# Attention, convolution and filter sums in a two-layer encoder: four steps placed elsewhere in the order

## The chip, the cores and the metric

The kernel runs on one core of one Trainium2 chip. The metric is device time in microseconds (us) of one execution. Engines: PE is TensorE (its weight loads are shown as PEld), DVE is VectorE, ACT is ScalarE, POOL is GpSimd, SP is SyncE, which issues DMAs; POOL issues DMAs too.

## What is computed

The reference runs layers (here two, DEPTH = 2) on 1024 tokens of width 1024, all in float32. Each layer does three sub-layers, each followed by a residual sum and a layer norm:

```python
proj = x @ w_in
# (A) grouped-query attention, 8 query heads of 64 over 2 key/value heads, rotary
# (B) gated long convolution, 256 channels, by FFT with a filter that an MLP makes
# (C) latent attention, 4 heads, low-rank keys and values, rotary part apart
x = layer_norm(alpha * x + concat(A, B, C) @ w_o)
x = layer_norm(alpha * x + cross_attention(x, mem))      # 4 heads of 256, 256 memory tokens
x = layer_norm(alpha * x + moe(x))                       # 16 experts, each takes its top tokens
```

The kernel keeps float32 accuracy by splitting each matrix into a high part (rounded by a copy on ACT) and a low part (the difference, a subtraction on DVE or POOL) and multiplying in three passes. `split` is that pair of instructions: L175 the copy, L176 the subtraction; L187 to L189 are the three passes of a product.

## The kernel before

**Order.** PE, ACT and DVE execute their instructions in the order in which the program text issues them (MANUAL, L31, and `manual_schedule`, L2009). POOL and SP are not in MANUAL; the build orders them.

**Attention** (`attention`, L572) is one software pipeline over both kinds of heads: 48 pairs of 128-token blocks, 32 of grouped heads and then 16 of latent heads, two iterations a pair, so 96 iterations and some to drain. Iteration n issues, in this order:
- `put` of the pair that was finished: three copies `olo` from PSUM on ACT (L566 to L568), a sum and a product on POOL (L569, L570)
- in every second iteration the reciprocal `rd` of the two columns of sums `den` of one pair (L585, DVE). Before, that is the pair whose second half of values comes in this iteration: pair q at iteration 2q + 6
- the scores S of block n (L527, four matmuls for a grouped head, six for a latent one) and their row maximum `nm` (L530, DVE)
- `turn(n - 3)`: eight transposes of the exponentials (L544), split into `PH` (ACT) and `PL` (DVE), the operands of the value products
- exp of the scores (L536, ACT), which also sums the row into `den` (a second instruction reads the accumulator)
- half the values of an earlier pair (L554, L555); with the second half, two transposes of `rd` (L558), which `put` multiplies by
- `side(n, 2)`: what runs beside attention

**Beside attention**, in the order of `side`: one step of the convolution (`hyena`, L1001) if HYP(n) holds; a load of latent-attention tiles (`back`, L718, POOL's DMA queue) at iterations 57 to 63, 70, 78 and 86; a load of an out-projection weight `wo` (SP's queue) at 84, 86, ..., 96 and 97. The loads: Q tiles `mq` of the first block pair at 57, K tiles `mk` at 58 to 61, V tiles at 62 and 63, the other Q tiles at 70, 78 and 86; scores 64 are the first that need K, and scores 72, 80 and 88 the first that need the Q of 70, 78 and 86.

**The convolution** has one step outside the pipeline and 55 in it. Steps 1 to 8 are transposes and products on PE, with splits. Steps 9 to 46 are sums and products on POOL. Steps 47 to 50 and 52 are concerned with the inverse transform: a split `abh` (ACT), `abl` (POOL) of one block, and the load of the next table `tab` (L804, POOL's DMA queue); step 47 also reloads two tiles and the first table. Steps 49, 51, 53, 54 and 55 hold matmuls of the inverse. With the HYP of before, step 1 is at iteration 4, step 46 at 71, step 47 at 73, steps 48 to 50 at 74, 76 and 77, and step 55 at 85.

**The out-projection** follows: `Weight.get` splits a weight tile into `woh` (ACT) and `wol` (on DVE for `wo[0]` and `wo[2]`, on POOL for `wo[1]` and `wo[3]`) when it is first taken, before this is in the out-projection's first block. `r` (L1201) is the residual sum.

**Cross attention** runs 13 iterations over four heads: queries, scores, exponentials `xE` (L1389, ACT), the reciprocal of their sums (L1391, DVE), the product with it (L1392, POOL), transposes (L1403) with splits `xPH` and `xPL`, values. In layer 0 it also has the sums of the second layer's filter (`filter_later`, L943 to L997, 15 steps on DVE with an occasional copy): two steps after each iteration from 3 to 10.

Of the kernel before, what the change touches and what calls it, by code (L numbers as in the profile page):

```python
# [33 lines left out]
ML0 = 1  # L34
FM = 14
AT0 = 14
HYP = lambda n: n > 2 and n % 3
UC = 1
UG = 3
EM = 8  # L40
# [97 lines left out]
class Net:  # L138
# [433 lines left out]
    def attention(self, n_pairs, pair, side, lead=3):  # L572


        its = [(n, i) for n in range(n_pairs) for i in range(2)]
        E, PT, den, O, late, out = {}, {}, {}, {}, [], []
        for n in range(len(its) + lead + 3):
            for q in out:
                tp, _, _, f = pair(q)
                self.put(O.pop(q), tp, f)  # L580
            out = []
            if late and late[0][1]:
                q = late[0][0]
                rd = self.sml(2, "rd")
                self.nc.vector.reciprocal(rd, den[q])  # L585
                den[q] = rd
            sc = None
            if n < len(its):
                p, i = its[n]
                tp, passes = pair(p)[:2]  # L590
                sc = self.scores(passes(tp * 2 + i))
            side(n, 0)
            m = n - lead
            if 0 <= m < len(its):
                p, i = its[m]
                if i == 0:
                    PT[p] = ([self.big((128, 4, 256), F32R, name="PH") for _ in range(2)],
                             [self.big((128, 4, 256), F32R, name="PL") for _ in range(2)])
                self.turn(E.pop(m), *PT[p], i)
            side(n, 1)  # L600
            if sc:
                p, i = its[n]
                if i == 0:
                    den[p] = self.sp.tile([128, 2], F32, tag="den", name="den", bufs=6)
                E[n] = self.exps(*sc, den[p][:, i:i + 1])
            if late:
                q, half = late.pop(0)
                if half == 0:
                    O[q] = self.psO()
                self.values(O[q], *PT[q], den[q], pair(q)[2], half)  # L610
                if half:
                    out.append(q)
                    del PT[q], den[q]
            if 0 <= m < len(its) and its[m][1]:
                late += [(its[m][0], 0), (its[m][0], 1)]
            side(n, 2)
            yield
# [1139 lines left out]
    def run(self):  # L1757
# [26 lines left out]
        n = 0  # L1784
# [11 lines left out]
        for l in range(DEPTH):  # L1796
# [3 lines left out]
            wo = []  # L1800
            gqa, (mla, back) = self.gqa(), self.mla(l)
            hy = self.hyena(l)
            later = self.filter_later() if l == 0 else iter(())

            def side(n, at):
                if at != 2:
                    return
                if HYP(n):
                    next(hy, None)
                if 57 <= n < 64 or n in (70, 78, 86):  # L1810
                    next(back, None)
                if n in (84, 86, 88, 90, 92, 94, 96, 97):
                    wo.extend(self.out_weights(A["w_o"][l], [len(wo)]))

            ATS = 0
            att = self.attention(48, lambda n: gqa[n]() if n < 32 else mla[n - 32], side)
            for n, _ in enumerate(proj, NT if l else 0):
                if n == NT - 1 + (l > 0):
# [62 lines left out]
            for n, _ in enumerate(cross):  # L1881
                if n in (6, 7, 8, 9):
                    wo2 += self.out_weights(A["xa_wo"][l], [2 * (n - 6), 2 * (n - 6) + 1])
                for _ in range(WG.get(n, 0)):
                    next(w for w in wo2 if w.parts is None).get()
                if n == 11:
                    next(pl)
                if n >= 3:
                    next(later, None)
                    next(later, None)  # L1890

            self.more = True
            self.ew, loads = [], self.expert_weights(l)
# [142 lines left out]
```

## Time and profile before

| | |
|---|---|
| median of 3 runs | 2730.91 us (2730.67 to 2734.1) |
| the profiled execution | 2730.33 us, span 2728.6 us |
| PE busy | 2540.0 us, 93% of the span |
| DVE, ACT, POOL busy | 1963.7, 1589.2, 830.0 us (72%, 58%, 30%) |
| attention, layer 0 | scores 0 at 344.4 us, scores 95 at 655.8 us |
| attention, layer 1 | scores 0 at 1660.6 us, scores 95 at 1972.3 us |
| granted clock of PE, mean | 0.972 of 2.4 GHz |

A row of a timeline gives start, length, engine, line, operation, what it writes and reads with shapes, how many instructions are merged, and in brackets the idle time just before it and what ended that idle time. Ends of matmuls are modelled, and instructions of an engine overlap a little: the next may start before the last has left the pipe, so that the distance of two starts is the safer measure.

### The profile page before, as it was taken

Reading aid. Unit: us, or ns where it says so; the run is one execution under the profiler, and the core shown is the slowest. Engines: PE = TensorE matmul, PEld = TensorE weight load, DVE = VectorE, ACT = ScalarE, POOL = GpSimd, SP = SyncE. Lnnn points to the kernel's source line nnn. Section 1 sums busy time; section 2 is a strip of 40 time slices with the busy share of each in tenths; the row PEclk is TensorE's granted clock in tenths of the full one; section 3 lists DMA queues with packets and bytes.
Section 4 is the critical chain, followed back from the end, with each engine's and each line's share of the span. In section 5 each row is a group of like instructions: output and inputs, shape, how many; then the busy total and the mean of one; then the engine's idle time right before and its main releaser. Section 6 shows DMA issues by size and latency. Waiting matters only on the chain.

```text
span 2728.6 us, 39209 instructions
## 1 busy us (share of the span) xinstructions
PE 2540.0 (93%) x14132; PEld 2138.4 (78%) x14132; DVE 1963.7 (72%) x3089; ACT 1589.2 (58%) x2828; POOL 830.0 (30%) x761
## 2 busy tenths in 40 slices
PE   7899989999999895999989998999989999599998
PEld 5688879988778784777869887999877888477775
DVE  6765578877645678889876556887765356889887
ACT  4743379988123443887854425998732344377885
POOL 2412427963101201121131333688230130011112
PEclk9899999999999996999999999999999999799999
DMA  7545100333233357999975610005323235699994
GB/s 196 192 161 200 28 24 17 75 100 120 86 109 118 121 187 252 351 378 371 342 241 171 208 60 24 9 24 140 94 85 101 85 101 185 239 340 372 377 344 154
DMA packets 222581, 462.76 MB, mean 170 GB/s; under 512 B 26298, under 2 KB 83216, under 8 KB 222386
## 3 DMA queue, kind: packets, MB, share of 16 engines
q1 hardware_dynamic: 198402, 374.56, 39.2%
q0 software_dynamic: 19376, 68.91, 9.5%
q10 hardware_dynamic: 4608, 16.78, 1.5%
q8 instruction: 111, 1.82, 0.3%
q14 instruction: 84, 0.69, 0.1%
HBM read 369.75 MB, written 90.44 MB: 169 GB/s over the span
## 4 chain that ended last, share of the span: by engine, by line
PE 70%; DVE 13%; issue 5%; ACT 5%; DMA 4%; POOL 2%; SPq 0%; ACTq 0%; DVEq 0%; POOLq 0%
PE S L187 7%; PE S L188 7%; PE S L189 7%; PE S L527 6%; PE O L1709 6%; PE T L544 5%; PE O L189 5%; PE O L188 5%; PE O L187 5%; PE S L421 4%; PE O L555 3%; PE O L554 3%; DVE rk L1512 2%; DMA eg<-moe_w_up 1%; PE T L1463 1%
## 5 line engine op out<-in xcount | busy, mean ns | idle before, releaser
L176 DVE TENSOR_TENSOR egl<-eg,egh 128x1024 fp32r<-128x1024 f32 x256 | 305.8, 1221 | 49.9 <-ACT egh L175 45.6
L530 DVE TENSOR_REDUCE nm<-S 128x1 f32<-128x1024 f32 x192 | 234.5, 1223 | 102.5 <-PE S L527 100.4
L175 ACT ACTIVATE egh<-eg 128x1024 fp32r<-128x1024 f32 x256 | 265.1, 1058 | 41.0 <-PE S L188 23.9
L176 DVE TENSOR_TENSOR PL<-T,PH 128x512 fp32r<-128x512 f32 x384 | 246.3, 683 | 17.4 <-ACT PH L175 14.2
L175 ACT ACTIVATE PH<-T 128x512 fp32r<-128x512 f32 x384 | 209.4, 595 | 69.0 <-PE T L544 67.6
L536 ACT ACTIVATE E<-S,nm 128x1024 f32<-128x1024 f32 x192 | 214.7, 1118 | 7.7 <-DVE nm L530 7.4
L187 PE MATMUL S<-woh,mh 128*128 128x512 f32 x512 | 207.9, 406 | 6.0 <-DVE r L1201 6.0
L544 PE MATMUL T<-ident,E 128*128 128x128 f32 x1536 | 203.4, 274 | 2.3 <-DVE PL L176 1.4
L188 PE MATMUL S<-wol,mh 128*128 128x512 f32 x512 | 202.1, 395 | 3.7 <-POOL wol L176 2.4
L544 PEld LDWEIGHTS T<-ident,E 128*128 128x128 f32 x1536 | 179.7, 141 | 32.2 <-DVE PL L176 4.0
L187 PE MATMUL S<-egh,xt 128*128 128x512 f32 x512 | 204.1, 399 | 0.0
L189 PE MATMUL S<-woh,ml 128*128 128x512 f32 x512 | 201.6, 394 | 0.0
L189 PE MATMUL S<-egh,xt 128*128 128x512 f32 x512 | 200.9, 392 | 0.0
L188 PE MATMUL S<-egl,xt 128*128 128x512 f32 x512 | 200.6, 392 | 0.0
L176 DVE TENSOR_TENSOR edl<-ed,edh 128x1024 fp32r<-128x1024 f32 x128 | 153.2, 1220 | 18.5 <-ACT edh L175 18.5
L1709 PE MATMUL O<-edh,ht 128*128 128x512 f32 x512 | 155.4, 406 | 1.4 <-ACT ht L175 1.4
L527 PE MATMUL S<-KS,QS 128*128 128x512 f32 x512 | 148.1, 413 | 1.6 <-ACT E L536 1.6
L1651 POOL DMA_INDIRECT xg<-x2d,ix x32 | 54.6, 1705 | 301.0 <-PE O L1709 143.0
L175 ACT ACTIVATE edh<-ed 128x1024 fp32r<-128x1024 f32 x128 | 132.4, 1055 | 22.8 <-PE S L188 13.2
L569 POOL TENSOR_TENSOR olo<-olo 64x256 f32<-64x256 f32 x96 | 70.3, 733 | 227.3 <-ACT olo L567 185.3
L554 PE MATMUL O<-PH,VS 128*128 128x256 f32 x512 | 137.9, 302 | 0.0
L1724 POOL DMA_INDIRECT yd<-ye,ix x31 | 49.1, 1583 | 260.9 <-ACT ye L1723 104.8
(438 smaller groups left out, 7093.1 us busy)
## 6 DMA issues: line engine op xcount, KB each, us to landing
eg<-moe_w_gate SPq DMA_DIRECT2D x128, 512.0 KB, 11.2
eg<-moe_w_up SPq DMA_DIRECT2D x128, 512.0 KB, 11.2
ed<-moe_w_down SPq DMA_DIRECT2D x128, 512.0 KB, 11.4
wv<-xa_wkv SPq DMA_DIRECT2D x16, 512.0 KB, 8.0
wk<-xa_wkv SPq DMA_DIRECT2D x16, 512.0 KB, 6.3
wo<-w_o SPq DMA_DIRECT2D x16, 512.0 KB, 3.5
x1d<-r SPq DMA_DIRECT2D x16, 512.0 KB, 2.6
wq<-xa_wq SPq DMA_DIRECT2D x16, 512.0 KB, 4.2
```

The source lines that it names most:

```text
L175: self.nc.scalar.activation(h, src, AF.Copy)
L176: (self.nc.vector if le == "v" else self.nc.gpsimd).tensor_sub(l, src, h.bitcast(F32))
L187: mm(out, ah, bh, start=start, stop=False)
L188: mm(out, ah, bl, start=False, stop=False)
L189: mm(out, al, bh, start=False, stop=stop)
L421: nc.tensor.matmul(P[:, hf * 512:hf * 512 + 512], a[:, k, :], self.half(b, hf, k), start=s, stop=e)
L527: self.nc.tensor.matmul(S[:, hf * 512:hf * 512 + 512], a, b[hf], start=n == 0, stop=n == len(passes) - 1)
L530: self.nc.vector.tensor_reduce(nm, S, axis=AX.X, op=OP.max, negate=True)
L536: self.nc.scalar.activation(E, S, AF.Exp, bias=nm, scale=1.0, accum_out=den)
L544: self.nc.tensor.transpose(pt[:, k, :], P[:, kt * 128:(kt + 1) * 128], self.ident)
L554: nc.tensor.matmul(O[:, :256], v, PH[half][:, k, :], start=kt == 0, stop=False)
L1709: nc.tensor.matmul(O[e][n], a[:, 2 * u + f, :], w[:, n * 512:n * 512 + 512], start=s, stop=z)
```

## The change

Four things:
- HYP, the iterations that carry a step of the convolution: all n > 2 that are not a multiple of 3 before, all n > 8 that are not a multiple of 4 after. Step 1 then is at iteration 9, step 8 at 18, step 37 at 57, steps 38, 39 and 40 at 58, 59 and 61, step 46 at 69, steps 47 to 50 at 70, 71, 73 and 74, step 52 at 77, step 55 at 81.
- The reciprocal of pair q is issued at the start of iteration 2q + 2, the one behind the pair's second exp, in place of 2q + 6.
- `wo[0]` to `wo[3]` are split (`get`) at iterations 90, 92, 94 and 96 of attention, in place of the out-projection's first block.
- The steps of `filter_later` are taken three at a time after iterations 3 to 7 of cross attention, in place of two at a time after iterations 3 to 10. Head 3, the last, begins its queries at iteration 8.

```diff
-HYP = lambda n: n > 2 and n % 3
+HYP = lambda n: n > 8 and n % 4
...
-            if late and late[0][1]:
-                q = late[0][0]
+            if 0 < n <= len(its) and its[n - 1][1]:
+                q = its[n - 1][0]
                 rd = self.sml(2, "rd")
                 self.nc.vector.reciprocal(rd, den[q])
                 den[q] = rd
...
                 if n in (84, 86, 88, 90, 92, 94, 96, 97):
                     wo.extend(self.out_weights(A["w_o"][l], [len(wo)]))
+                if n in (90, 92, 94, 96):
+                    wo[n // 2 - 45].get()
...
-                if n >= 3:
-                    next(later, None)
-                    next(later, None)
+                if 3 <= n < 8:
+                    for _ in range(3):
+                        next(later, None)
```

## Rows read from the trace of the kernel before

**Rows 1.** Busy time by stretch: stretch, length, PE, PEld, DVE, ACT, POOL, granted clock, DMA.
```profile
440.00:540.00 100.00, 100.00 (x736) 92.16 (x735) 87.07 (x123) 92.97 (x193) 85.64 (x83) 1.00 0.19 50
```

**Rows 2.** Waits of PE, 656 to 692 us: who for whom, total us, times, longest.
```profile
PE O L558 <- DVE rd L585: 2.7, 1, 2.7
...
PE S L188 <- POOL wol L176: 1.2, 3, 0.6
```

**Rows 3.** Busy time by stretch: cross attention's last head, layers 0 and 1.
```profile
888.00:931.00 43.00, 34.69 (x168) 28.41 (x166) 25.77 (x31) 17.09 (x38) 10.03 (x5) 0.92 0.27 92
...
2205.54:2237.66 32.12, 30.47 (x167) 25.95 (x165) 15.55 (x23) 15.93 (x37) 8.76 (x4) 1.00 0.27 83
```

**Rows 4.** Busy time by stretch: behind the wait for xE in layer 0.
```profile
913.90:917.30 3.40, 3.40 (x14) 2.92 (x12) 1.38 (x3) 2.65 (x10) 1.38 (x1) 0.51 0.00 0
```

**Rows 5.** Timeline, DVE, layer 0's cross attention, head 1.
```profile
845.35 2.80 DVE L945 TENSOR_TENSOR X<-X 128x1024 f32<-128x1024 f32 x1
```

**Rows 6.** Timeline, DVE, end of layer 0's attention.
```profile
669.11 1.26 DVE L176 TENSOR_TENSOR PL<-T,PH 128x512 fp32r<-128x512 f32 x2
```

**Rows 7.** Timeline, ACT, grouped heads, layer 0.
```profile
447.66 1.12 ACT L536 ACTIVATE E<-S,nm 128x1024 f32<-128x1024 f32 x1
...
450.78 1.11 ACT L536 ACTIVATE E<-S,nm 128x1024 f32<-128x1024 f32 x1
...
451.78 0.20 ACT L536 ACTIVATION_READ_ACCUMULATOR E<-S,nm 128x1 f32 x1
...
453.38 1.12 ACT L536 ACTIVATE E<-S,nm 128x1024 f32<-128x1024 f32 x1
...
456.65 1.12 ACT L536 ACTIVATE E<-S,nm 128x1024 f32<-128x1024 f32 x1
```

**Rows 8.** Timeline, DVE, a reciprocal and what follows it.
```profile
844.01 0.18 DVE L1391 RECIPROCAL xrd<-xden 128x4 f32<-128x4 f32 x1 [2.08 <-ACT xE L1389]
844.11 1.21 DVE L943 TENSOR_TENSOR bf<-X 128x1024 f32<-128x1024 f32 x1
```

**Rows 9.** Timeline, DVE, grouped heads, layer 0.
```profile
451.97 1.23 DVE L530 TENSOR_REDUCE nm<-S 128x1 f32<-128x1024 f32 x1
```

**Rows 10.** Timeline, PE, grouped heads, layer 0.
```profile
450.85 1.09 PE L527 MATMUL S<-KS,QS 128*128 128x512 f32 x4
...
456.58 1.09 PE L527 MATMUL S<-KS,QS 128*128 128x512 f32 x4
```

**Rows 11.** Timeline, PE, scores 77 and 80 of layer 0.
```profile
587.57 0.63 PE L527 MATMUL S<-mk,mq 96*128 96x512 f32 x2
...
600.68 1.88 PE L527 MATMUL S<-mk,mq 96*128 96x512 f32 x6 [0.92 <-DMA mq<-ld]
```

**Rows 12.** Timeline, POOL, iterations 77 and 78 of layer 0.
```profile
592.92 2.42 POOL L176 TENSOR_TENSOR abl<-Z,abh 128x1024 fp32r<-128x1024 f32 x1 [2.14 <-ACT abh L175]
...
595.85 1.04 POOL L718 DMA_DIRECT2D mq<-ld  x2
```

**Rows 13.** Instructions of tile mq, 560 to 606 us: time from issue to landing.
```profile
DMA to landing us min/median/max: 4.0/4.6/5.4
```

**Rows 14.** Timeline, PE, scores 70 and 72 of layer 0.
```profile
562.52 1.56 PE L527 MATMUL S<-mk,mq 96*128 96x512 f32 x6
...
569.24 1.69 PE L527 MATMUL S<-mk,mq 96*128 96x512 f32 x6
```

**Rows 15.** Timeline, POOL, iteration 73 of layer 0.
```profile
578.11 2.39 POOL L176 TENSOR_TENSOR abl<-Z,abh 128x1024 fp32r<-128x1024 f32 x1 [1.50 <-issue]
```

**Rows 16.** Timeline, POOL, loads of K in layer 0.
```profile
535.71 0.51 POOL L718 DMA_DIRECT2D mk<-ld  x1
```

**Rows 17.** Instructions of tile mk, 534 to 541 us: time from issue to landing.
```profile
DMA to landing us min/median/max: 3.9/4.9/6.7
```

**Rows 18.** Timeline, PE, scores 64 of layer 0.
```profile
542.55 1.55 PE L527 MATMUL S<-mk,mq 96*128 96x512 f32 x6
```

**Rows 19.** Timeline, PE, convolution's first transposes in layer 0's attention.
```profile
362.87 0.71 PE L1023 MATMUL T<-ident,zx 128*128 128x128 f32 x4 [0.98 <-DVE PL L176]
```

## The prediction

> **What bounds the kernel now.** I read the page's busy shares first (TensorE is busy 93% of the span), then TensorE's idle time by what ended it, then the loops of attention instruction by instruction. In the steady part of attention TensorE never idles: busy 100.00 of 100 us, with ACT at 92.97, DVE at 87.07 and POOL at 85.64 [rows 1]. So time can be won only where TensorE idles, and is lost wherever one of these nearly full engines comes to answer later. The idle places near the change are two. At the end of attention and in the out-projection, TensorE waits 2.7 us for `rd` and three times, together 1.2 us, for a `wol` from POOL, in layer 0 [rows 2]; a fourth wait, for a `wol` from VectorE, is as long as the longest of these, 0.6, and one for `r` follows. Layer 1 has the same waits. In the last head of layer 0's cross attention, 43.00 us hold 168 matmuls; the same piece of layer 1, which has no filter sums, holds 167 in 32.12 us [rows 3]: 10.9 us. The longest idle in it is for `xE`, which POOL multiplies by a reciprocal that waits on VectorE behind four sums. The granted clock falls behind that wait: 0.51 over 3.40 us, the lower level, 1.2 GHz [rows 4]. Work done in such a stretch takes twice as long, so 3.4 us of it cost 1.7 us.
>
> **Filter sums apart from the last head.** Steps 1 to 15 of `filter_later` now come three at a time after iterations 3 to 7, before it was two after 3 to 10. What layer 1 shows without them is the upper bound of the gain, -10.9 us [rows 3]; I take 10.8, as the two pieces differ by a matmul. Against it, iterations 3 to 6 carry one more step each. These sums are VectorE instructions of 0.7 to 1.2 us, and one beside POOL took 2.80 us [rows 5]. The splits `xPL` of head 1 stand behind the sums on VectorE, and the next transposes need the PSUM that they free; they move back by some three us of extra sums, while TensorE has query projections for about one. I take 3 us of new idle and 1.5 us of lower clock: -10.8 + 4.5 = **-6.3 us**. Bounds: -10.8 (all hidden) to -1 (twice the cost).
>
> **Reciprocals and out-projection splits, at the tail.** With `rd` ready long before, the 2.7 us wait [rows 2] doesn't vanish. The next late thing is `PL` of the last iteration: its two splits start at 669.11 and take 1.26 [rows 6], right behind the reciprocal. What brings `PL` forward is the `wol` split of 1.2 us that no longer stands ahead of it on VectorE. Gain there about 1. The four waits for `wol` (1.8 us, with the refill of the pipe behind each 2.9) go, since these splits are done inside attention. The wait for `r` stays, some 0.3 less. The splits cost in turn about 0.3 us inside iterations 90 and 94 (VectorE, latent heads) and delay the last iteration's turns; I worked this into -3.9 a layer, and half a us of clock comes on top. Both layers: **-8.8 us**, bounds -4 (new splits hold up turns) to -12 (every wait of rows 2 but the last goes).
>
> **Reciprocals, in the steady loop.** This is a new wait, and it comes 48 times a layer. Before, the reciprocal of pair q ran four iterations after its sums and never waited. Now it stands directly behind the second exp of its pair, on VectorE, and ahead of `nm` of the next iteration. The order on PE, ACT and DVE is the program's (MANUAL), so `nm` can't pass it. That closes a ring: exp (odd) -> its accumulator read -> reciprocal -> nm (even) -> exp (even) -> three olo copies and two PH -> exp (odd). Its time, from rows: exp start to end of its read 451.98 - 450.78 = 1.20 us [rows 7]; the reciprocal holds up the instruction behind it by 0.10 us [rows 8]; `nm` takes 1.23 [rows 9]; from its end to exp 0.18 (453.38 - 453.20) [rows 7, 9]; a few hundredths for the semaphore. Sum 2.74. From exp (even) to exp (odd) it is ACT alone without idle time, 456.65 - 453.38 = 3.27, and 450.78 - 447.66 = 3.12 in the pair before [rows 7]; mean 3.20. The ring takes 5.94 us a pair. TensorE's own pitch is 456.58 - 450.85 = 5.73 [rows 10]. The ring becomes the bound by about 0.19 us a pair. In the latent heads (pitch 6.7) and where convolution matmuls fill TensorE it isn't; some 24 grouped pairs a layer are left: 24 x 0.19 x 2 = **+9.1 us**. Bounds: 0 (the ring is 0.2 shorter than its records say) to +14 (0.22 over all 32 pairs).
>
> **Convolution from iteration 9.** Its 55 steps now go three in four iterations, before two in three. So they begin five iterations later, end four earlier, and are shifted against the loads of the latent heads, which stay at iterations 57 to 63, 70, 78 and 86. Those are issued by POOL, which also does most of the steps (about 2.5 us each).
> Step 47 (first split of the inverse tables) was at 73, after the load of Q tiles at 70; it now stands at 70, just ahead of that load. Ahead of it on POOL's queue are then a table, `abl`, the next table. `abl` waits for ACT's `abh`, which stands behind exp. The pattern is in the trace at iterations 77 and 78: scores at 587.57 [rows 11], `abl` at 592.92 after 2.14 us of idle for `abh`, the next table, Q's loads at 595.85 [rows 12], and the scores of iteration 80 started at 600.68 after 0.92 us of idle for them [rows 11]. So Q is issued 595.85 - 587.57 = 8.3 us after the iteration's scores. At 70 it is needed two iterations on: scores 70 start at 562.52, scores 72 at 569.24, 6.72 us [rows 14]. A load lands 4.0 to 5.4 us after its issue, median 4.6 [rows 13]: at 12.3 to 13.1 for the first of the two tiles, the second half a us behind it and needed later. TensorE waits some 6.1 us; a clock stretch behind it adds 1.4 (1.7, not certain). 7.5 us a layer. The Trainium skill ("DMA: Bandwidth & Descriptors", section on the anatomy of one DMA on the SWDGE path) fits such a transfer as 2.0 us and the bytes at 436 GB/s; for 384 KB that is an estimate of 2.9 us, by which the wait would be 1 to 2 us shorter a layer; the landings above disagree, and the sum goes by them.
> Whether POOL keeps that order is open: POOL and SP aren't in MANUAL, the build orders them. For it speaks that POOL idled 1.50 us ahead of the `abl` at 578.11 [rows 15], while the next table's load, which depends on nothing there, stayed behind it.
> The other effects: the last K tile that scores 64 need was issued at 535.71 [rows 16], landed 6.7 us later, the longest [rows 17], and the scores started at 542.55 [rows 18], 0.15 us after that. It gets one more step of about 2.5 us ahead of it: +1.7 a layer (0 to 3). The wait for Q at iteration 80 [rows 11] goes in both layers, -0.9 each, as more matmuls stand ahead of these scores and no table is queued there. At the start some -0.9 a layer, as the convolution's first transposes no longer wait 0.98 us for `PL` [rows 19]. Sum: 2 x (7.5 + 1.7 - 0.9 - 0.9) = **+14.8 us**; bounds -4 (Q not held up, K in time) to +22.
>
> **Sum.** -6.3 - 8.8 + 9.1 + 14.8 = +8.8 us. The profiled execution took 2730.33 us (span 2728.6), the median of the runs is 2730.91: **2739 us**. About 0.2%, 5.5 us, is what a measurement of this kernel can tell from no change.
>
> **The rivals.**
> *Q loads aren't held up* (chance 0.18): the build issues them ahead of `abl`. Then 2 x 7.5 goes: 2724. For it: nothing in the data makes them wait. Against: rows 15.
> *The ring doesn't bind* (0.15): the reciprocal fits in the slack between nm and exp. Then 9.1 goes: 2730. For it: ACT idles 7% of rows 1. Against: that idle time lies in the half of the ring that grows from about 2.5 to 2.74.
> *Both* (0.04): 2715.
> *The filter sums cost in heads 1 and 2 what they cost in the last* (0.08), on the slower side: three sums stand ahead of `xPL` in each of iterations 3 to 7, and from 4 us of idle in two of them on the gain is gone: 2739 + 6 to 8, 2746.
> That the change doesn't do what it says I give no share of its own: program order on VectorE settles the reciprocals, and loads of the splits are issued six iterations ahead of the first.
>
> **How the numbers follow.** The forecast itself has 0.55, with 2731 to 2747 as its own range. Range 2719 to 2748: it takes in most of the first two rivals, leaving out about 0.05 above and 0.09 below. Slower by over 0.2% (above 2736.4): 0.55 x 0.68 + 0.08 + 0.02 = 0.48. Within 0.2%: 0.165 of the forecast, 0.07 of the first rival, 0.105 of the second, 0.34. Faster: the rest, 0.18.
>
> **What would show it.** Queue: TensorE idle for `mq` at iteration 72 of both layers, 5 to 7 us, then a granted clock near 0.5; none means the first rival. Ring: a pair of grouped heads takes 5.9 us in place of 5.73, TensorE's busy share in the stretch of rows 1 falls to about 97%, the reciprocal's idle is ended by ACT. Tail: waits for `rd` and `wol` gone, one for `PL` of 1 to 2 us in their place. Filter: last head of layer 0 near 32 us, with a new wait for `xPL` in head 1 or 2. I am wrong above all if Q's load passes `abl`, or if nm and exp leave the ring 0.2 us that the records don't show.

## The result, and the profile after

The changed kernel takes 2749.64 us (median of 4 runs, 2747.93 to 2752.13), the kernel before 2732.51 beside it (2730.67 to 2735.89): a ratio of 1.0062, 95% interval 1.0045 to 1.0079, 17 us slower. The profiled execution's span grew from 2728.6 to 2746.1 us. Forecast was 2739, range 2719 to 2748: the way was right, the forecast rise of 8 us is half of the measured one, and the time lies just above the range.

TensorE has the same 14132 matmuls and is busy for the same time (2540.8 us, before 2540.0). The 17.5 us are idle time, nearly all of it (a matmul at the lower clock counts as busy, and such stretches came and went). Where they arise can be read by setting the start of the same matmul in both traces side by side; the table gives how much later (+) the changed kernel is, piece by piece.

| piece (us later in the changed kernel) | forecast, both layers | layer 0 | layer 1 |
|---|---|---|---|
| scores 0 to 24: the convolution begins later | -1.8 | +0.1 | -0.6 |
| scores 24 to 62: the ring of the reciprocals | +9.1 | +1.5 | +1.8 |
| scores 62 to 66: K | +3.4 | +1.8 | +1.7 |
| scores 66 to 89: Q at 72, Q at 80 | +13.2 | +7.9 | +8.4 |
| scores 89 to the last value products | in the next | +3.1 | +1.0 |
| from there to the end of the out-projection | -8.8 | -5.0 | -4.8 |
| cross attention: the filter sums | -6.3 | +0.6 | 0.0 |

The pieces sum to +17.4 before rounding; -0.6 ahead of layer 0's attention and +0.7 between and behind, where nothing was changed, make it 17.5. That stretch ahead of attention is the same code in every kernel here, and yet its length differs by -1.3 to +2.9 us from that of before among their traces. So differences of a few us are read below from a place inside attention on, where the time alone doesn't settle them. Not every place is equally sharp. In traces of kernels with the same code there, scores 24 to 66 take 121.50 to 121.53 us, but scores 0 to 24 take 81.9 to 83.3, scores 66 to 89 differ by up to 0.6, and scores 89 to the last value products by up to 1.4.

First, the steady part of attention (columns as in [rows 1]):

```profile
440.00:540.00 100.00, 99.47 (x721) 90.09 (x722) 86.24 (x123) 94.55 (x192) 89.18 (x83) 1.00 0.14 40
```

Where TensorE was busy 100.00 of 100 us [rows 1], it is busy 99.47, with 721 matmuls in place of 736. The waits of TensorE from 570 to 700 us, which answer to [rows 2] (who for whom, total us, times, longest):

```profile
PE S L527 <- DMA mq<-ld: 6.7, 1, 6.7
PE T L544 <- DVE PL L176: 2.7, 2, 1.7
PE O L555 <- DVE PL L176: 2.1, 1, 2.1
PE S L187 <- DVE r L1201: 1.8, 1, 1.8
...
```

The waits for `rd` and `wol` [rows 2] are gone. In their place stand 2.7 us at the last turns and 2.1 us at the last values, both for `PL`, and ahead of all that the 6.7 us for `mq`. The last head of cross attention in layer 0, in the same view, first two rows of before (888 to 931 us) and then the changed kernel (890 to 935 us):

```profile
PE T L1403 <- POOL xE L1392: 4.6, 1, 4.6
PE O L187 <- DVE xo L181: 2.4, 1, 2.4
...
```

```profile
PE O L187 <- ACT wqh L175: 6.0, 1, 6.0
PE T L1403 <- POOL xE L1392: 1.0, 1, 1.0
PE O L187 <- ACT xo L183: 0.7, 1, 0.7
```

`xE` took 4.6 us there before (the longest idle of the piece in [rows 3]); now it takes 1.0, as in layer 1, and the wait of 2.4 us for `xo` is gone, but a wait of 6.0 us for `wqh` has come that neither layer had.

### The profile page after: what moved, and what is told of

Its sections match the earlier page's. It is cut to its first block, busy times and chain, and to the rows that moved or that the text cites. A ratio compares the mean times of both kernels' runs of the same rounds, so it can differ in the third digit from the quotient of the medians.

```text
span 2746.1 us, 39184 instructions
## 1 busy us (share of the span) xinstructions
PE 2540.8 (93%) x14132; PEld 2136.6 (78%) x14132; DVE 1959.6 (71%) x3089; ACT 1593.7 (58%) x2828; POOL 829.3 (30%) x761
## 4 chain that ended last, share of the span: by engine, by line
PE 45%; DVE 10%; DMA 5%; ACT 4%; issue 4%; POOL 1%; ACTq 0%; SPq 0%; DVEq 0%; POOLq 0%
PE S L187 6%; PE S L188 6%; PE S L189 5%; PE O L1709 5%; PE S L527 3%; PE O L187 3%; PE O L189 3%; PE O L188 2%; PE T L544 2%; PE S L421 2%; DMA eg<-moe_w_gate 2%; DVE rk L1512 1%; DMA eg<-moe_w_up 1%; PE O L555 1%; PE O L554 1%
## 5 line engine op out<-in xcount | busy, mean ns | idle before, releaser
L544 PE MATMUL T<-ident,E 128*128 128x128 f32 x1536 | 209.1, 277 | 7.4 <-DVE PL L176 6.5
```

The costliest lines, as they stand in the source:

```text
L544: self.nc.tensor.transpose(pt[:, k, :], P[:, kt * 128:(kt + 1) * 128], self.ident)
```

## The experiments

The stated ratio of each is to the kernel before, run beside it on the same chip.

### Each part alone

Four kernels make one part of the change each.

**Convolution.** The edit is the first line of the diff:

```diff
-HYP = lambda n: n > 2 and n % 3
+HYP = lambda n: n > 8 and n % 4
```

> The convolution's new iterations alone, the rest as before. Theory (POOL's queue): the whole loss of attention is here. At scores 72 TensorE waits 6.6 us for mq in both layers and loses about 1.9 more at the lower clock, 1.3 a layer goes at scores 64, 0.9 a layer comes back at scores 80: +17 us or more. Rival (sum of parts): the stall needs the reciprocals too, because only a late exp pushes abh back; then the wait for mq is under 4 us and the kernel under +10.

Measured: 2751.94 us against 2730.76, ratio 1.0078 (1.0061 to 1.0095), +21 us. TensorE's waits from 570 to 600 us:

```profile
PE S L527 <- DMA mq<-ld: 6.4, 1, 6.4
```

The stall for `mq` is there without the reciprocals, at nearly its full length (in layer 1 it is 6.9 us). So the theory holds, and the convolution's new place alone costs more than the whole change; the other parts give 4 us back.

**Filter.**

```diff
-                if n >= 3:
-                    next(later, None)
-                    next(later, None)
+                if 3 <= n < 8:
+                    for _ in range(3):
+                        next(later, None)
```

> The filter sums' new iterations alone. Theory (SP's queue): the gain of the last head is given back by the load of its second query weight, which stands behind the stores of the filter on SP: TensorE waits about 6 us for wqh, 2 us for xPL in head 2, and the time is within 2 us of before. Rival (VectorE only): the wait for wqh is under 1 us and the kernel 5 to 8 us faster.

Measured: 2731.76 against 2730.76, ratio 1.0008 (0.9998 to 1.0017): no difference. TensorE's waits in layer 0's cross attention, 845 to 930 us:

```profile
PE O L187 <- ACT wqh L175: 5.9, 1, 5.9
PE T L1403 <- DVE xPL L176: 2.0, 1, 2.0
PE T L1403 <- POOL xE L1392: 1.0, 1, 1.0
...
```

What is won at `xE` is lost at `wqh`. The 2.0 us for `xPL` are the wait that the prediction had put at 3.

**Reciprocals.**

```diff
-            if late and late[0][1]:
-                q = late[0][0]
+            if 0 < n <= len(its) and its[n - 1][1]:
+                q = its[n - 1][0]
```

> The reciprocals alone. Theory (ring of 5.77 us): a pair of grouped heads takes 5.76 in place of 5.73, 1 us a layer, and at the end the wait for rd of 2.7 gives way to one for PL of 2 or more: 0 to +2 us in all. Rival (the ring as the prediction had it, 5.94): pairs of 5.9, +8 us or more.

Measured: 2734.33 against 2730.76, ratio 1.0014 (1.0004 to 1.0023), +3.6 us, 1.6 us above what the theory gave and far from the rival's 8. From scores 34 to 56 of layer 0 a pair takes 5.79 us, before 5.73. Scores 24 to 62 of both layers take 2.3 us more. Scores 66 to 89 take 0.75 us more in each layer, too, but that is little above the scatter there. TensorE's waits from 655 to 700 us:

```profile
...
PE O L554 <- ACT PH L175: 1.8, 1, 1.8
PE S L188 <- POOL wol L176: 1.2, 3, 0.6
PE O L555 <- DVE PL L176: 0.9, 1, 0.9
PE T L544 <- DVE PL L176: 0.7, 1, 0.7
```

The 2.7 us for `rd` have turned into 1.8 for `PH` and 0.9 for `PL`, just as long together: at the end the operands of the last turn come no sooner, whatever `rd` does.

**Splits.**

```diff
+                if n in (90, 92, 94, 96):
+                    wo[n // 2 - 45].get()
```

> The out-projection splits inside attention alone. Theory: the out-projection gains 5 us a layer (four waits and the lower clock), the last iterations of attention lose 1 to 3: -4 to -8 us in all. Rival (the splits delay rd as well, which still stands behind them): the loss at the end of attention eats it, within 2 us of before.

Measured: 2724.99 against 2730.76, ratio 0.9980 (0.9971 to 0.9990), -5.8 us, as the theory had it. TensorE's waits from 655 to 700 us:

```profile
PE T L544 <- DVE PL L176: 2.4, 2, 1.4
PE O L558 <- DVE rd L585: 2.1, 1, 2.1
...
```

No wait for `wol` is left, and 1.7 us more are spent at `PL` than before (2.4; the same view of before has 0.7).

The four differences, +21.2, +1.0, +3.6 and -5.8, sum to +20; together they make +17. Most of it is the convolution's.

### Three mends of the changed kernel

Each leaves the four parts of the change in place and takes away what the trace shows as the cause of one loss. The kernel before took 2730.78 us beside these three and 2732.51 beside the changed kernel. So a difference of times to the changed kernel carries 1.7 us of that; what the traces show at the place itself is given with it.

**Q's load first.** Here is POOL's queue at iteration 70 of the changed kernel, and the scores that wait for it, those of iteration 72 (scores 70 start at 565.38 there):

```profile
568.49 0.58 POOL L804 DMA_DIRECT2D tab<-k_idft  x1
570.61 2.37 POOL L176 TENSOR_TENSOR abl<-Z,abh 128x1024 fp32r<-128x1024 f32 x1 [1.55 <-ACT abh L175]
572.95 0.57 POOL L804 DMA_DIRECT2D tab<-k_idft  x1
573.51 1.03 POOL L718 DMA_DIRECT2D mq<-ld  x2
...
578.88 2.90 PE L527 MATMUL S<-mk,mq 96*128 96x512 f32 x6 [6.69 <-DMA mq<-ld]
```

The table, `abl` with 1.55 us of idle for `abh`, the next table, and only then `mq`, 8.1 us after the scores. The instructions of tile `mq` in this stretch give the time from issue to landing:

```profile
DMA to landing us min/median/max: 5.2/5.7/6.1
```

and the stretches behind the wait, in layer 0 and in layer 1, give the granted clock (the third number from the end):

```profile
578.90:583.10 4.20, 4.20 (x14) 3.51 (x15) 1.22 (x1) 0.43 (x1) 0.03 (x1) 0.50 0.54 134
1904.25:1910.90 6.65, 6.65 (x25) 5.90 (x26) 2.61 (x3) 2.29 (x4) 0.09 (x1) 0.50 0.31 87
```

First landing 5.2 us after the issue, where [rows 13] had 4.0 to 5.4; then 4.20 us at 0.50, which is 1.2 GHz, and in layer 1 as much as 6.65.

```diff
+                if n == 70:
+                    next(back, None)
                 if HYP(n):
                     next(hy, None)
-                if 57 <= n < 64 or n in (70, 78, 86):
+                if 57 <= n < 64 or n in (78, 86):
                     next(back, None)
```

> The changed kernel, with Q's load of iteration 70 issued ahead of the convolution's step of that iteration; nothing else. Theory (POOL's queue): the wait for mq at scores 72 falls from 6.7 us to under 1 in both layers, the stretch at the lower clock goes: 16 to 17 us faster than the changed kernel, about before's time. Rival (the load is slow because the tables' loads share the DMA engines, or the tile's buffer comes free late): a wait of 2 us or more stays.

Measured: 2732.49 against 2730.78, ratio 1.0009 (0.9999 to 1.0018): 17 us faster than the changed kernel, by one load ahead of one step. The traces show 17.6 us of it between scores 66 and 89 of the two layers, wait and clock together. POOL's queue now, in the same place:

```profile
568.34 1.05 POOL L718 DMA_DIRECT2D mq<-ld  x2
569.38 0.57 POOL L804 DMA_DIRECT2D tab<-k_idft  x1
570.99 2.39 POOL L176 TENSOR_TENSOR abl<-Z,abh 128x1024 fp32r<-128x1024 f32 x1 [1.04 <-ACT abh L175]
```

The wait of 6.7 us is gone in layer 0, 0.6 are left in layer 1. This also tells the prediction's main rival from the forecast: POOL keeps the program's order here.

**The weight first.** SP's queue (SPq) and TensorE in the last head of the changed kernel:

```profile
880.35 0.33 SPq L968 DMA_DIRECT2D fd<-Z  x1
880.73 1.26 SPq L127 DMA_DIRECT2D wo<-xa_wo  x2
893.67 2.73 SPq L968 DMA_DIRECT2D fd<-Z  x3
896.51 0.46 SPq L127 DMA_DIRECT2D wq<-xa_wq  x1
...
905.70 0.79 PE L187 MATMUL O<-xh,wqh 128*128 128x512 f32 x1 [5.96 <-ACT wqh L175]
```

`fd` are the stores of the filter (L968). Three of them stand on SP until the sums `Z` are done; the load `wq` of the last head's second query weight is issued behind them, at 896.51, and the split and the matmuls wait for it until 905.70. TensorE then works some 5 us at a granted clock of 0.50. The load was slow besides: it landed 8.0 us after its issue, the two weights before it after 3.6 and 3.4. By these numbers a landing after 3.4 us would have left a wait of about 1.4 us of the 6.0 (an estimate). So the place in the queue and the slow landing act together; no run here separates them.

```diff
             if hf == 0 and n < 7 and n + 1 not in ws:
                 ws[n + 1] = load((n + 1) // 2, (n + 1) % 2)
+            if n == 5 and hf == 0:
+                ws[7] = load(3, 1)
```

> The changed kernel, with the load of the last head's second query weight issued together with the first's, ahead of the filter's stores. Theory (SP's queue): the wait of 6.0 us for wqh goes and 6 to 8 us of the changed kernel's time with it. Rival (the DMA engines are busy with K, V and the stores): the wait stays over 2 us.

Measured: 2739.99 against 2730.78, ratio 1.0042 (1.0026 to 1.0058), 9.6 us less than the changed kernel (8.5 in cross attention of layer 0, by the traces), a little more than the theory's 6 to 8. TensorE's waits of the same stretch:

```profile
PE T L1405 <- POOL xE L1394: 1.0, 1, 1.0
PE O L187 <- ACT xo L183: 0.7, 1, 0.7
```

What is left are the two waits of layer 1; the 2.0 us for `xPL` stay, in an earlier head. The stretch at the lower clock behind the wait is gone, too. From the queries of layer 0's cross attention to its end the kernel gains 8.0 us on the kernel before, where the changed kernel lost 0.6. So the filter's new place does pay, once no load stands behind its stores.

**The splits earlier.** The end of the changed kernel's attention, on DVE:

```profile
669.06 1.22 DVE L176 TENSOR_TENSOR wol<-wo,woh 128x1024 fp32r<-128x1024 f32 x1 [1.03 <-ACT woh L175]
670.20 1.22 DVE L530 TENSOR_REDUCE nm<-S 128x1 f32<-128x1024 f32 x1
671.34 1.28 DVE L176 TENSOR_TENSOR PL<-T,PH 128x512 fp32r<-128x512 f32 x2
...
677.83 3.71 DVE L176 TENSOR_TENSOR ml<-mix,mh 128x512 fp32r<-128x512 f32 x3
681.47 1.27 DVE L176 TENSOR_TENSOR PL<-T,PH 128x512 fp32r<-128x512 f32 x2
```

`wol` of iteration 94 stands ahead of `nm`, and it has itself waited 1.03 us for ACT's `woh`; `nm`, the last exponentials and `PL` all come behind it. (The three `ml` splits ahead of the last `PL` were there before, too, ahead of the `PL` in [rows 6].)

```diff
-                if n in (90, 92, 94, 96):
-                    wo[n // 2 - 45].get()
+                if n in (86, 88, 90, 92):
+                    wo[n // 2 - 43].get()
```

> The changed kernel, with wo[0] to wo[3] split at iterations 86, 88, 90 and 92 in place of 90, 92, 94 and 96. Theory (the split at 96 stands among the last turns on ACT and POOL): the two waits for PL of 1.7 and 1.0 us at the last turns fall by half or more, 1.5 to 4 us a layer faster. Rival (the out-projection's own ml splits set the end): less than 1 us a layer.

Measured: 2741.13 against 2730.78, ratio 1.0042 (1.0027 to 1.0056), 8.5 us less than the changed kernel, 4 a layer, at the theory's upper end (9.0 by the traces, from scores 89 to the end of the out-projection of both layers). TensorE's waits, 655 to 700 us:

```profile
...
PE T L544 <- DVE PL L176: 1.0, 2, 0.7
PE O L555 <- DVE PL L176: 0.3, 1, 0.3
```

`PL` costs 1.3 us in all in place of 4.8. Which of the four splits did the harm was not separated.

### Together, and what the rest is worth

**All three mends**, with the loads first at every iteration of `side`, and the splits and the weight as above:

```diff
-                if HYP(n):
-                    next(hy, None)
                 if 57 <= n < 64 or n in (70, 78, 86):
                     next(back, None)
+                if HYP(n):
+                    next(hy, None)
```

> The changed kernel with three places mended at once: every load of K, V and Q issued ahead of the convolution's step of its iteration (57 to 63, 70, 78, 86), the last head's second query weight loaded with the first, wo[0] to wo[3] split from 86 to 92. Theory (three separate places, each its own queue): the gains add, -17 - 9 - 8 and -2 to -4 for K at scores 64, so 2709 to 2716, 15 to 22 us faster than before. Rival (what one gives is taken by the next): no faster than before by more than 8.

Measured: 2717.64 against 2730.02, ratio 0.9955 (0.9938 to 0.9971), 12 us faster than before. This lies between the theory's 15 to 22 and the rival's 8. The gains of the three mends, 17 + 10 + 8.5, sum to 35 from the changed kernel, and 32 came, K's loads included (2.5 us by the traces). With each time taken against the kernel before beside it, the three give 15.4, 7.9 and 6.8, which is 30, and all together 29.5. So they add but for a few us; some of what is missing is a wait for `mq` that is back at scores 72, of 0.9 us in layer 0 and 1.3 in layer 1.

**Reciprocals outside the ring.**

```diff
-            if 0 < n <= len(its) and its[n - 1][1]:
-                q = its[n - 1][0]
+            if 3 <= n < len(its) + 3 and its[n - 3][1]:
+                q = its[n - 3][0]
```

> The same, with the reciprocal of pair q at iteration 2q + 4, two iterations behind its sums: rd is still early at the end, but no exp has just been issued when it is. Theory (ring): 1 us a layer from the grouped heads and up to 0.8 from the latent ones come back, 2 to 4 us faster than the kernel with the reciprocal at 2q + 2. Rival (the ring isn't what costs there): the same within 1 us.

Measured: 2712.55 against 2730.02, ratio 0.9935 (0.9918 to 0.9951), 5 us faster than with the reciprocal at 2q + 2, a little more than the theory said. From scores 34 to 56 a pair takes 5.73 us again, as before; in the changed kernel 5.77 in layer 0 and 5.80 in layer 1. Between scores 24 and 62 of both layers the trace is 3.3 us shorter than that of the kernel with all three mends.

**The convolution where it was**, the rest as in the last kernel (HYP and `side` as before the change):

> The kernel with the reciprocal at 2q + 4, the weight load and the early splits, but the convolution's iterations and the order of loads of before. It tells what the convolution's place is worth once no load stands behind it. Theory (nothing: its matmuls and sums cost the same at either place): within 3 us of the kernel with the later iterations. Rival (the waits of 0.9 and 1.2 for Q at 80 and those at the start count): 3 to 6 us slower.

Measured: 2708.95 against 2730.02, ratio 0.9921 (0.9904 to 0.9937). That is 3.6 us faster than the kernel with the later iterations, a little more than the theory's 3, and the other way from the rival's. The two traces differ by 4.2 us in all, but as much already at scores 0, ahead of everything that was changed. The sharp piece settles it: from scores 24 to 66 the kernel with the later iterations takes about 1.25 us longer in each layer, 0.7 of it up to scores 62 and 0.5 from there. The convolution's later place costs about 2.5 us, then, even with its loads in order; it gains nothing here.

**Reciprocals of before**, the rest as in the last kernel:

```diff
-            if 3 <= n < len(its) + 3 and its[n - 3][1]:
-                q = its[n - 3][0]
+            if late and late[0][1]:
+                q = late[0][0]
```

> The kernel of e10_conv_before with the reciprocals where they were before (iteration 2q + 6), so it differs from the kernel before only by the filter's iterations with the weight loaded early, and by the splits at 86 to 92. It tells what early reciprocals are worth when they are outside the ring. Theory (PL is late next): the wait for rd comes back at the end of attention, 1 to 3 us a layer, 2 to 5 us slower than e10_conv_before. Rival (with the splits gone from there VectorE is free, rd isn't late): the same within 1 us.

Measured: 2708.61 against 2730.72, ratio 0.9919 (0.9902 to 0.9935): the same as with early reciprocals. The rival holds. TensorE's waits, 655 to 695 us, here and (last line) the one that stands in the early reciprocal's kernel in place of `rd`:

```profile
PE S L187 <- DVE r L1201: 1.8, 1, 1.8
PE T L544 <- DVE PL L176: 0.7, 1, 0.7
PE O L558 <- DVE rd L585: 0.3, 1, 0.3
```

```profile
PE O L555 <- DVE PL L176: 0.4, 1, 0.4
```

DVE's rows of the kernel before, just ahead of the `PL` in [rows 6]:

```profile
665.00 1.23 DVE L176 TENSOR_TENSOR wol<-wo,woh 128x1024 fp32r<-128x1024 f32 x1
666.14 2.96 DVE L176 TENSOR_TENSOR ml<-mix,mh 128x512 fp32r<-128x512 f32 x3
669.03 0.15 DVE L585 RECIPROCAL rd<-den 128x2 f32<-128x2 f32 x1
```

Most of the 2.7 us for `rd` had come from the out-projection's splits there: `wol` stood in front of it on DVE, and the three `ml` behind `wol` took 2.96 us, where they take 1.88 with the split gone. Now `rd` is late by 0.3 us where it was, and `PL` by 0.4 where it is early. So the two fastest versions, at 2709 us, are the same within what these runs can tell, and the second needs only two parts of the change, each with one place mended: the splits (at 86 to 92) and the filter sums (with the weight loaded first).

**The ring, lengthened.** The changed kernel's ring in the grouped heads (ACT, then DVE; answers to [rows 7 to 9]):

```profile
451.53 1.11 ACT L536 ACTIVATE E<-S,nm 128x1024 f32<-128x1024 f32 x1
452.53 0.20 ACT L536 ACTIVATION_READ_ACCUMULATOR E<-S,nm 128x1 f32 x1
...
454.10 1.12 ACT L536 ACTIVATE E<-S,nm 128x1024 f32<-128x1024 f32 x1 [0.20 <-DVE nm L530]
...
457.36 1.12 ACT L536 ACTIVATE E<-S,nm 128x1024 f32<-128x1024 f32 x1
...
452.76 0.17 DVE L585 RECIPROCAL rd<-den 128x2 f32<-128x2 f32 x1 [0.27 <-ACT E L536]
452.84 1.22 DVE L530 TENSOR_REDUCE nm<-S 128x1 f32<-128x1024 f32 x1
```

exp (odd) at 451.53, its read over at 452.73, the reciprocal at 452.76 with `nm` 0.08 behind it, and exp (even) at 454.10, which this time waited 0.20 us for `nm`: 2.57 us, and 3.26 from there to the next. If this ring is the bound, longer reciprocals lengthen each pair.

```diff
-                self.nc.vector.reciprocal(rd, den[q])
+                for _ in range(3):
+                    self.nc.vector.reciprocal(rd, den[q])
```

> The reciprocals alone, as in e3_recip, but each issued three times. If the ring over exp, reciprocal and nm is the bound of the grouped heads, as e3_recip reads (pairs of 5.77 us), two more reciprocals of about 0.08 us lengthen each pair by 0.16: pairs of 5.93, 4 to 5 us a layer, 8 to 10 us more than e3_recip. If the 1 us a layer has another cause, nothing changes by more than 2.

Measured: 2754.17 against 2730.02, ratio 1.0087 (1.0070 to 1.0104), 20 us more than one reciprocal. From scores 34 to 56 a pair takes 6.16 us. DVE's rows:

```profile
456.07 0.57 DVE L586 RECIPROCAL rd<-den 128x2 f32<-128x2 f32 x3 [0.22 <-ACT E L536]
456.55 1.20 DVE L530 TENSOR_REDUCE nm<-S 128x1 f32<-128x1024 f32 x1
```

Three reciprocals hold `nm` up by 0.48 us, not by the 0.24 that three times 0.08 would be: all three write the same tile, and by their length together (0.57, one takes 0.17) they start 0.20 us apart; `nm` starts 0.08 behind the last. The ring grows by 0.40, and every pair by nearly as much (5.79 to 6.16), which is why the loss is twice the 8 to 10 us expected. The ring is the bound, at either length.

## Why the prediction was half right

**The way and the largest term: right.** Q's load at iteration 70 was held up as forecast, behind a table, `abl` and the next table, since POOL kept the program's order. Forecast: issue 8.3 us after the scores, landing 4.0 to 4.8, wait 6.1, clock 1.4. Measured: 8.1, 5.2, 6.7 (layer 1: 6.6); and the stretch at 0.50 costs half its length, 2.1 us in layer 0 and 3.3 in layer 1. So the size of the clock term was off most: 5.4 us of both layers for 2.8. The landing was at the upper end of [rows 13]; the forecast took 4.0 to 4.8, where the load of its own pattern, the one behind a table at 595.85, had 4.8. By the fit in "DMA: Bandwidth & Descriptors" of the Trainium skill (section on the anatomy of one DMA on the SWDGE path), such a load is an estimate of 2.9 us; this trace disagrees here too, with 5.2 and 6.1. K at scores 64 cost 1.8 and 1.7 us, forecast 1.7.

**The filter sums: the step that failed.** Forecast -6.3, measured +0.6. Both halves of its working were right in kind (the wait for `xE` goes, one for `xPL` of 2 us comes). What is missing in it is a queue: the step that was moved also issues DMAs, the stores `fd` on SP. The last three moved from iterations 9 and 10 to 7, and so to a place ahead of a weight's load that iteration 8 issues, in SP's queue, where they wait for VectorE. The prediction followed VectorE alone. The cost that it did foresee, 4.5 us in the earlier heads, is 2.0 in the changed kernel's trace; a stretch at the lower clock follows that wait only in some traces of the same code (3.4 us from 855.3 with the filter's part alone). The rival named for this part (sums in front of `xPL` cost as much as they gain) had nearly the right price with the wrong mechanism. The kernel with the weight loaded early shows it: the piece then gains 8.0 us, and the kernel takes 9.6 us less than the changed one.

**The ring: right mechanism, size wrong.** Forecast 0.19 us a pair and +9.1, measured +3.3 from scores 24 to 62 of both layers, and there the convolution alone takes 1.1 (with the reciprocals alone it is 2.3). Two terms of the sum were read wrongly. From the end of `nm` to exp I took 0.18 us out of [rows 7, 9]; in that row exp had no idle time ahead of it, it was ACT's own `PH` that set its start, and where exp does wait for `nm` it is 0.04 (452.84 + 1.22 to 454.10). The reciprocal holds `nm` up by 0.08, not 0.10. With 2.57 in place of 2.74, and the mean of 3.20, the ring is 5.77 us against TensorE's 5.73: it binds by 0.04, not by 0.19. TensorE's busy share, about 97% by the forecast, is 99.47%. The experiments with three reciprocals and with none in the ring show that the ring does bind.

**The tail: half right.** The out-projection gained 5 us a layer, more than the 3.7 or so that the forecast had for it: four waits, their refill and, in layer 0, the stretch at the lower clock behind `r` (3.4 us from 688.7). That stretch was not saved, though: the changed kernel has one at the last value products (3.4 us from 682.1), so that part of the gain comes back as a loss of the end of attention. In all, the end of attention lost 3.1 and 1.0 us where I had a gain of about 1: the splits at 90 to 96 cost more than 0.3 (the scatter of that piece is up to 1.4). The step at fault is that I priced only their length on DVE; `wol` waits for ACT's `woh`, and everything behind it on DVE (`nm`, `PL`) waits with it. Moving them four iterations earlier brought 8.5 us. And that `rd` would no longer be late was worth nothing, as `PL` is late by as much; that part was said, though the reason for the lateness, the split in front, is gone by the other edit alone.

**The start** (-1.8 forecast) came out at -0.5. That isn't told from nothing: scores 0 to 24 take 81.9 to 83.3 us in the traces of kernels without the change there, 81.8 to 83.4 in the others with the convolution from iteration 9 and one reciprocal a pair.

In all: 8.8 forecast, 17.5 in the trace. The filter took 6.9 more than forecast, the tail 3.1 more, Q 3.1 more, the start 1.3 more, the ring 5.8 less. The forecast was as near as it was because the ring's error went the other way, and that was luck.

## What to carry to other kernels

When a step is moved, list every queue on which it issues anything, and for each queue what now stands behind it: two of the three large losses here were loads behind an instruction that waited for another engine, one on POOL and one on SP, and either vanished when the load was issued first. A wait that is removed at the end of a chain gives nothing while an operand of the same instruction is late by as much. And a latency read from two rows counts only if the later row shows that it waited; without idle time ahead of it, its own engine set its start.

## What was not expected of the hardware

A reciprocal of 128x2 let the instruction behind it start 0.08 us later, but three in a row into the same tile started 0.20 us apart (0.48 from the first to `nm`).

Loads of Q (384 KB, two at a time from POOL's queue) landed after 3.7 to 4.7 us where no table's load stood just ahead of them (before at iteration 70, Q's load first, the changed kernel at iteration 78), and after 4.8 to 6.1 where one did (before at iteration 78, the convolution alone and the changed kernel at iteration 70). What else was in flight was not taken apart.

The load of the weight behind three stores on SP landed 8.0 us after its issue; without stores in front, the load of the weight before it took 3.4.
